# Gathered expert rows fetched three ahead into five buffers and taken earlier, with attention's keys in a pool of their own

## The chip, the cores and the metric

One core of one Trainium2 chip runs one decoder layer for 512 prompt positions and 8 x 8 sampled positions. The metric is the device time of one execution in microseconds (us). Three runs of the kernel before took 1851.71, 1856.73 and 1860.59 us; the median is 1856.73 us.

## The reference, cut to what matters

The layer has two halves. The first projects the input, runs a short convolution and a windowed attention side by side, merges both with sigmoid gates, and normalizes. The second retrieves experts: for each token 8 heads pick 16 of 16384 experts, and each expert is one row of `expert_u` (1024 numbers, a dot product with the token) and one row of `expert_v` (added to the output with a weight).

```
z = x @ w_in                     -> conv inputs, q, k, v, two gates
merged = sigmoid(g_conv) * (conv @ w_conv_out) + sigmoid(g_attn) * (attn @ w_attn_out)
h = layer_norm(ALPHA * x + merged @ w_o)
s = (h @ w_pq) . sub_keys        -> top 16 of each half, top 16 of the sums: idx, gate
coef = gate * gelu(h . expert_u[idx])
out = layer_norm(ALPHA * h + sum(coef * expert_v[idx]))
```

## The kernel before, in words

Five chunks of tokens are worked in two waves. Wave 0 (`first`) holds chunk 0 (128 prompt positions) and chunk SMP (64 sampled tokens, and 64 prompt positions whose experts go with chunk 3). Wave 1 (`second`) holds chunks 1, 2 and 3 with 128, 128 and 64 rows. Every weight table of 128x1024 goes through `table` (L136): one DMA to `raw`, the rounded part `whi` on ACT (L119), the rest `wlo` on POOL or DVE (L120), and three matmuls for each product (L123 to L125).

The stages in order of time are: wave 0 up to its norm; wave 1's queries, keys, convolution and attention, mixed with wave 0's top-16 search (`ORDER`, L62); wave 1's merges, `merge_conv` (L648, eight gated products written to `br` at L662) and `merge_attention` (L664, eight more, then `w_o` and the norm at L190 to L200); wave 1's search (`scores`, L733, 16 blocks of `w_pq`, each group followed by five `front`s); the gate matrix (L774, 96 `hot` tiles on DVE at L787, DMA to `gd`); and the dense experts.

The two groups of tokens find their experts in different ways. For wave 1's 384 rows (`DENSE`) all 128 tables of `expert_u` are multiplied (`front(t)`, L856), the first 60 results are spilled to DRAM, the last ten fronts before the gate matrix is finished (`KEEP`) are held back until the last `hot` matmul, and then `middle(t)` and `back(t)` (L898, L916) multiply by the gate matrix and accumulate 18 matmuls a table into six PSUM banks `acc` (L940). Fronts 69 to 127 run inside that last loop. For the chunks in `GATHER` (0 and SMP) the rows are gathered: `experts()` (L491) is a generator of 384 steps, 192 on `eu` and then 192 on `ev`. A step issues one indirect DMA of 512 KB from POOL (L512) into the ring of `GBUF` tiles `g`, `GLAG` steps ahead, and one DVE instruction on the row that has landed: L526 for `eu` (dot product into `pre`), L535 for `ev` (added to `h_tok`). From the end of wave 1's merges until the gate matrix is done, L526 reads the token's copy `hp` in PSUM (L486) and later `h` in SBUF. The PSUM of `hp` and of the other search tiles is closed at L889, and `acc` is opened in its place.

How many steps run when is set by `side(n)` behind a table's split: none in wave 1's search blocks, alternately 2 and 1 behind each front up to front 68, 1 behind each table of the back loop up to t = 59, 3 from t = 60, and what is left at the end. Instructions are put in order on each engine by a scheduler, so an engine takes them in one fixed order and waits at the head of its queue. Pools on one side of SBUF are a stack; a tile that is opened where a closed pool lay waits for that pool's last readers. The attention's `kT_all`, `v_all` and `mask_p` are constants here; `br` of wave 1 lies where wave 0's search input was.

Of the kernel before, what the change touches and what calls it, by code (L numbers as in the profile page):

```python
# [23 lines left out]
SEQ = 512  # L24
# [27 lines left out]
NS = 60  # L52
LAG = 9
AHEAD = NS + LAG
GBUF = 4
GLAG = 2
RAW = dict(w=3, v=3)
HI = dict(w=4, v=2)
OB = 3


ORDER = "qkscscasacsca"  # L62
# [1 line left out]
KEEP = 10  # L64
# [1 line left out]


PACE_N = 18
PACE_A, PACE_B, PACE_U, PACE_V = (1, 0), (2, 1, 1), (2, 1), (1, 3)
LO_N = 50  # L70
GATED = "aaag"
OUT = "aaav"
# [3 lines left out]
def step_kernel(ctx: ExitStack, tc: tile.TileContext, I: dict, O: dict):  # L76
    nc = tc.nc
    V, A, G, PE, S = nc.vector, nc.scalar, nc.gpsimd, nc.tensor, nc.sync

    pools = {}  # L80

    def pool(key, side, bufs=1):
        return tc.tile_pool(name=key, bufs=bufs, side=side)
# [8 lines left out]
    def psum(name, bufs):  # L92
        return tc.tile_pool(name=name, bufs=bufs, space=bass.MemoryType.PSUM)
# [8 lines left out]
    def tmp(p, shape, tag, name=None, bufs=1, dt=F32):  # L102
        return pools[p].tile(shape, dt, tag=tag, name=name or tag, bufs=bufs)

    loads, newest = [], [None, None]
# [6 lines left out]
    def const(name, shape, dtype=F32, src=None):  # L112
        t = pools["c"].tile(shape, dtype, tag=name, name=name)
        if src is not None:
            loads.append((t, src))
        return t
# [19 lines left out]
    def table(src, p, eng, pace=0):  # L136
        raw = tmp(p, [128, 1024], "raw", bufs=RAW[p])
        newest[0] = S.dma_start(raw, src).ins
        hi = tmp(p, [128, 1024], "whi", bufs=HI[p], dt=F32R)
        lo = tmp(p, [128, 1024], "wlo", bufs=HI[p], dt=F32R)  # L140
        last = split(hi, lo, raw, eng)
        if pace:
            with tc.issue_after(last.ins):
                side(pace)
        return hi, lo
# [14 lines left out]

    ident = const("ident", [128, 128])
    make_identity(nc, ident)
    mask_p = const("mask_p", [128, 256], src=I["mask_p"])
    convw = const("convw", [128, 4, 3], src=I["conv_w"])
    sink_p = const("sink_p", [128, 8], src=I["sink_p"])
    sink_s = const("sink_s", [128, 2, 2], src=I["sink_s"])
# [3 lines left out]
    ucar = const("ucar", [128, 4, 2])  # L170
    V.memset(ucar, 0.0)
    state = const("state", [128, 4, 8, 2], src=I["state"])
    kT_all = const("kT_all", [128, SEQ])
    v_all = const("v_all", [128, 5, 128])

    iota128 = const("iota128", [128, 128], src=I["iota128"])
    h_tok, idx, gate = {3: const("h3", [128, D])}, {}, {}
# [313 lines left out]
    def experts():  # L491
# [14 lines left out]
        def row():  # L506
            return tmp("g", [128, D], "g", bufs=GBUF)

# [5 lines left out]

        for i in range(GLAG):
            fetch(i)
        yield
        for i, (src, c, s) in enumerate(jobs):
            if i + GLAG < len(jobs):
                fetch(i + GLAG)  # L520
            g = rows.pop(i)
# [53 lines left out]
    def load_x(s):  # L575
        i, (a, b) = next(s.pieces)
        raw = tmp("g", [128, 1024], "g", bufs=GBUF)[:, :(b - a) * s.mv]
        S.dma_start(raw, I[f"xT{s.w}"][:, a * s.mv:b * s.mv])
        split(s.xT[0][:, a:b, :], s.xT[1][:, a:b, :], raw.rearrange("p (k n) -> p k n", n=s.mv), G if i == 1 else V)

    def weight(s, src):
        s.units += 1
        if s.w == 0:
            return table(src, "w", G if s.units % 3 != 1 else V)
        if s.units > LO_N:
            return table(src, "w", G)
        pace = PACE_A if s.units <= PACE_N else PACE_B
        if s.units % 4 == 3:
            return table(src, "w", V)
        return table(src, "w", G, pace[s.units % len(pace)])  # L590
# [35 lines left out]
    def attention(s, i):  # L626
# [7 lines left out]
        if c == SMP:  # L634
            kc = tmp("g", [128, 8, 128], "g", name="kc", bufs=GBUF)
            late(kc, I["kcT"])
            vc = tmp("g", [128, 8, 128], "g", name="vc", bufs=GBUF)
            late(vc, I["vc"])
# [171 lines left out]
    ks, bs = ExitStack(), ExitStack()  # L810
    pools["k"] = ks.enter_context(pool("k", "left"))
    pools["mm"] = ks.enter_context(psum("mm", 3))
    at_stack = ExitStack()
    pools["at"] = at_stack.enter_context(psum("at", 3))
    sel3 = ([tmp("k", [128, 128], f"k3{k}") for k in range(2)], tmp("k", [128, 128], "gt3"))
# [15 lines left out]
    for x in ORDER:  # L831
        do[x]()
        count[x] += 1
    first.rs.close()
    for dst, src in zip((*sel3[0], sel3[1]), (*first.sel[1][0], first.sel[1][1])):
        V.tensor_copy(dst[64:128], src[64:128])
    keys = {c: first.sel[i][0] for i, c in enumerate(GATHER)}
# [11 lines left out]
    scratch.append(shared[0])  # L849
    pools["hp"] = ks.enter_context(psum("hp", 1))  # L850
    pools["f"] = ctx.enter_context(pool("f", "right"))
    pools["b"] = bs.enter_context(pool("b", "right"))
    hT = second.hT
    coef = {}

    def front(t):  # L856
        wu = table(I["euT"][t], "w", G if t < AHEAD else V, PACE_U[t % len(PACE_U)] if t < AHEAD else 0)
        ps = bank("u")
        for k in range(8):
            mm3(ps[:, :ND], block(wu, k), (hT[0][:, k, :], hT[1][:, k, :]), k == 0, k == 7)  # L860
        if t < NS:
            ge = tmp("f", [128, ND], "sp", bufs=2)
            A.activation(ge, ps[:, :ND], AF.Gelu)  # L863
            S.dma_start(spill[t], ge)
        else:
            ge = tmp("f", [128, ND], "gel", bufs=LAG)
            A.activation(ge, ps[:, :ND], AF.Gelu)
            coef[t] = ge
# [3 lines left out]
    def fronts(n):  # L872
        nonlocal done
        while done < min(n, NE):
            front(done)
            done += 1

    for k, g4 in enumerate((0, 2, 1, 3)):
        scores(second, g4)
        fronts(FQ * (k + 1))  # L880
    total = len(DENSE) * 128 // GN
    base = done
    for i in range(len(DENSE)):
# [168 lines left out]
```

## Time and profile before

| what | us |
|---|---|
| median of three runs | 1856.73 |
| the profiled execution's own time | 1850.18 |
| its span, first to last instruction | 1848.4 |
| PE busy / DVE busy / POOL busy / ACT busy | 1723.9 / 1464.7 / 1109.6 / 781.4 |
| mean granted TensorE clock (share of full) | 0.972 |

The share of PE (93%) is a mean over stages with different limits, so a stage has to be read from its own stretch of the span. The profiled execution is 6.55 us under the median of the runs.

### The profile page before, as it was taken

The numbers are of one execution on the slowest core, as the hardware profiler recorded it, in microseconds if no ns is written. First come the engines' busy times: TensorE is split into PE (matmuls) and PEld (weight loads), VectorE is DVE, ScalarE is ACT, GpSimd is POOL, SyncE is SP. The second block draws the span as 40 slices with busy tenths as digits, with TensorE's granted clock in tenths as the row PEclk, the third lists the DMA queues.
The fourth block names the chain that finished last, engine by engine and source line by source line (L and its number), as shares of the span: only waits on it lengthen the run. The fifth ranks groups of instructions, "written<-read, shape, count | busy, mean of one in ns | idle before, by whom it ended". The sixth has DMA issues, their size and how long they took to land.

```text
span 1848.4 us, 27569 instructions
## 1 busy us (share of the span) xinstructions
PE 1723.9 (93%) x9760; PEld 1566.4 (85%) x9760; DVE 1464.7 (79%) x2588; ACT 781.4 (42%) x1337; POOL 1109.6 (60%) x724
## 2 busy tenths in 40 slices
PE   7999998998799999899888899999999999999985
PEld 7998898988489899799878778778999999999974
DVE  5634579998965699987893778779788878888887
ACT  4554444443233344377794333333333333343322
POOL 4445434367857777798645422224678787778783
PEclk9999999999989999899999999999999999999998
DMA  7446443368757789899748899999999999989873
GB/s 252 134 150 225 138 132 122 115 200 300 249 201 241 235 294 311 271 349 348 289 188 303 317 333 335 336 346 339 333 314 345 337 324 350 353 307 343 314 268 104
DMA packets 190539, 496.50 MB, mean 269 GB/s; under 512 B 17712, under 2 KB 83696, under 8 KB 187312
## 3 DMA queue, kind: packets, MB, share of 16 engines
q1 hardware_dynamic: 135104, 293.39, 46.5%
q0 software_dynamic: 55296, 201.35, 30.2%
q8 instruction: 76, 1.25, 0.3%
q14 instruction: 63, 0.52, 0.1%
HBM read 454.48 MB, written 40.54 MB: 268 GB/s over the span
## 4 chain that ended last, share of the span: by engine, by line
PE 40%; DVE 23%; DMA 14%; issue 9%; POOL 8%; ACT 4%; SPq 1%; DVEq 0%; POOLq 0%; ACTq 0%
PE acc L940 15%; PE ps L123 7%; PE ps L124 7%; PE ps L125 7%; DMA g<-in_ev,idx 5%; POOL wlo L120 4%; POOL g L512 4%; DVE junk L526 3%; PE ps L796 3%; DMA re<-spill 2%; DVE wlo L120 2%; DMA raw<-in_ev 2%; DMA raw<-in_w_o 1%; ACT whi L119 1%; ACT hot L793 1%
## 5 line engine op out<-in xcount | busy, mean ns | idle before, releaser
L120 POOL TENSOR_TENSOR wlo<-raw,whi 128x1024 fp32r<-128x1024 f32 x232 | 579.1, 2499 | 301.8 <-ACT whi L119 264.7
L119 ACT ACTIVATE whi<-raw 128x1024 fp32r<-128x1024 f32 x388 | 409.5, 1056 | 603.9 <-PE ps L124 236.1
L123 PE MATMUL ps<-xhi,whi 128*128 128x384 f32 (+2 forms) x1600 | 529.9, 331 | 21.6 <-ACT sp L863 13.4
L125 PE MATMUL ps<-xhi,wlo 128*128 128x384 f32 (+2 forms) x1600 | 526.1, 329 | 3.5 <-POOL wlo L120 2.0
L124 PE MATMUL ps<-xlo,whi 128*128 128x384 f32 (+2 forms) x1600 | 526.1, 329 | 0.0
L535 DVE SCALAR_TENSOR_TENSOR h<-g,pre,h 128x1024 f32<-128x1024 f32 x192 | 309.8, 1614 | 68.3 <-DMA g<-in_ev,idx 66.8
L512 POOL DMA_INDIRECT g<-in_eu,idx x192 | 204.2, 1063 | 233.1 <-DVE junk L526 186.9
L123 PEld LDWEIGHTS ps<-xhi,whi 128*128 128x128 f32 x1600 | 308.4, 193 | 31.0 <-ACT sp L863 15.1
L512 POOL DMA_INDIRECT g<-in_ev,idx x192 | 257.0, 1338 | 124.9 <-DVE h L535 77.9
L125 PEld LDWEIGHTS ps<-xhi,wlo 128*128 128x128 f32 x1600 | 307.8, 192 | 5.3 <-POOL wlo L120 2.3
L124 PEld LDWEIGHTS ps<-xlo,whi 128*128 128x128 f32 x1600 | 308.3, 193 | 2.9 <-issue 0.3
L940 PE MATMUL acc<-whi,chi 128*128 128x512 f32 x756 | 291.4, 392 | 14.5 <-ACT chi L119 8.2
L940 PE MATMUL acc<-wlo,chi 128*128 128x512 f32 x756 | 296.9, 393 | 7.6 <-POOL wlo L120 7.6
L940 PE MATMUL acc<-whi,clo 128*128 128x512 f32 x756 | 256.4, 392 | 1.1 <-DVE clo L120 1.1
L120 DVE TENSOR_TENSOR wlo<-raw,whi 128x1024 fp32r<-128x1024 f32 x156 | 203.5, 1304 | 46.0 <-ACT whi L119 43.6
L940 PEld LDWEIGHTS acc<-whi,chi 128*128 128x128 f32 x756 | 142.6, 189 | 46.7 <-ACT chi L119 11.5
L940 PEld LDWEIGHTS acc<-wlo,chi 128*128 128x128 f32 x756 | 142.4, 188 | 38.0 <-POOL wlo L120 9.7
L526 DVE SCALAR_TENSOR_TENSOR junk<-g,hp 128x1024 bf16<-128x1024 f32 x104 | 125.9, 1210 | 56.8 <-DMA g<-in_eu,idx 54.8
L940 PEld LDWEIGHTS acc<-whi,clo 128*128 128x128 f32 x756 | 142.4, 188 | 31.3 <-DVE clo L120 1.6
L526 DVE SCALAR_TENSOR_TENSOR junk<-g,h 128x1024 bf16<-128x1024 f32 x88 | 130.9, 1488 | 3.3 <-DMA g<-in_eu,idx 3.0
L796 PE MATMUL ps<-hot 128*128 128x128 f32 x768 | 113.4, 290 | 14.5 <-ACT hot L793 13.4
L787 DVE TENSOR_TENSOR hot<-pt,T 128x1024 f32<-128x1024 f32 x96 | 113.9, 1218 | 15.8 <-PE ps L796 12.7
(250 smaller groups left out, 2157.9 us busy)
## 6 DMA issues: line engine op xcount, KB each, us to landing
raw<-in_euT SPq DMA_DIRECT2D x128, 512.0 KB
raw<-in_ev SPq DMA_DIRECT2D x128, 512.0 KB
gd<-gb SPq DMA_DIRECT2D x24, 1024.0 KB
gm<-gd SPq DMA_DIRECT2D x48, 512.0 KB
raw<-in_w_g SPq DMA_DIRECT2D x32, 512.0 KB
raw<-in_w_pq SPq DMA_DIRECT2D x32, 512.0 KB
raw<-in_w_bch SPq DMA_DIRECT2D x24, 512.0 KB
spill<-sp SPq DMA_DIRECT2D x60, 192.0 KB
```

What stands on the lines that cost most here:

```text
L119: A.activation(hi, src, AF.Copy)
L120: return (eng or V).tensor_tensor(lo, src, hi.bitcast(F32), op=ALU.subtract)
L123: PE.matmul(ps, L[0], R[0], start=start, stop=False)
L124: PE.matmul(ps, L[0], R[1], start=False, stop=False)
L125: PE.matmul(ps, L[1], R[0], start=False, stop=stop)
L512: G.indirect_dma_start(out=rows[i], out_offset=None, in_=I[src], in_offset=bass.IndirectOffsetOnAxis(ap=idx[c][:, s:s + 1], axis=0))
L526: V.scalar_tensor_tensor(junk, g, 1.0, in_psum(c), op0=ALU.mult, op1=ALU.mult, accum_out=p)
L535: V.scalar_tensor_tensor(h_tok[c], g, p, h_tok[c], op0=ALU.mult, op1=ALU.add)
L787: V.tensor_tensor(hot, iota_ps.unsqueeze(1).unsqueeze(1).broadcast_to([128, 2, 4, 128]), T[:, 0:2, n:n + 4].unsqueeze(3).broadcast_to([128 ...
L793: A.activation(oi, oi, AF.Copy, scale=weight_of)
L796: newest[1] = PE.matmul(ps[:, r * 128:(r + 1) * 128], hot[:, 1, r, :], oi, start=True, stop=True).ins
L940: PE.matmul(*args, **kw)
```

## The change

Four things are done.

1. The ring of gathered rows has five tiles instead of four, and rows are fetched three steps ahead instead of two. The `hot` tiles go from three to four.
2. One step is added behind each of the 16 `w_pq` blocks of wave 1's search (`PACE_Q`), and the ten fronts that are kept back carry 3 steps each instead of 2 or 1: 16 and 15 steps earlier, 31 in all. The back loop keeps its paces, so it runs out of steps earlier.
3. `mask_p`, `kT_all` and `v_all` move from the constants to a pool `kv` that opens before wave 0 and closes when wave 1's attention is over.
4. The search's score tiles `sc` of wave 1 get a pool `b0`, closed before the gate matrix opens `b`.

```diff
-GBUF = 4
-GLAG = 2
+GBUF = 5
+GLAG = 3
-OB = 3
+OB = 4
-PACE_A, PACE_B, PACE_U, PACE_V = (1, 0), (2, 1, 1), (2, 1), (1, 3)
+PACE_A, PACE_B, PACE_Q, PACE_U, PACE_V = (1, 0), (2, 1, 1), 1, (2, 1), (1, 3)
-    mask_p = const("mask_p", [128, 256], src=I["mask_p"])
-    kT_all = const("kT_all", [128, SEQ])
-    v_all = const("v_all", [128, 5, 128])
         if s.units > LO_N:
-            return table(src, "w", G)
+            return table(src, "w", G, PACE_Q)
+    kvs = ExitStack()
+    pools["kv"] = kvs.enter_context(pool("kv", "left"))
+    mask_p, kT_all = tmp("kv", [128, 256], "mask_p"), tmp("kv", [128, SEQ], "kT_all")
+    v_all = tmp("kv", [128, 5, 128], "v_all")
+    loads.insert(0, (mask_p, I["mask_p"]))
     first.rs.close()
+    kvs.close()
-    pools["b"] = bs.enter_context(pool("b", "right"))
+    pools["b"] = bs.enter_context(pool("b0", "right"))
-        wu = table(I["euT"][t], "w", G if t < AHEAD else V, PACE_U[t % len(PACE_U)] if t < AHEAD else 0)
+        wu = table(I["euT"][t], "w", G if t < AHEAD else V, (PACE_U[t % len(PACE_U)] if t < AHEAD - KEEP else 3) if t < AHEAD else 0)
+    bs.close()
+    pools["b"] = bs.enter_context(pool("b", "right"))
```

Up to the fourth gate product of wave 1's `merge_conv` PE has the same order in both kernels. Behind it PE takes the last attention (chunk 3: transposes L297, sums L134, output L311). Here are its second transposes before; a matmul with 128x320 is a product of the merge.

```order
L124 MATMUL ps<-xlo,whi 128x320
L297 MATMUL ps<-ident,t_4083 128x64
L297 MATMUL ps<-ident,t_4083 64x64
L125 MATMUL ps<-xhi,wlo 128x320
L297 MATMUL ps<-ident,t_4083 128x64
L297 MATMUL ps<-ident,t_4083 64x64
L123 MATMUL ps<-xhi,whi 128x320
L124 MATMUL ps<-xlo,whi 128x320
L297 MATMUL ps<-ident,t_4083 128x64
L297 MATMUL ps<-ident,t_4083 64x64
```

The same transposes (now L294) on PE in the changed kernel, up to the next product of the merge:

```order
L294 MATMUL ps<-ident,t_4086 128x64
L294 MATMUL ps<-ident,t_4086 64x64
L131 MATMUL ps<-v_all,t_4105 64x64
L134 MATMUL ps<-v_all,t_4105 64x64 x7
L308 MATMUL ps<-ident,o 128x64 x4
L123 MATMUL ps<-chi,whi 128x320
L124 MATMUL ps<-clo,whi 128x320
```

Before, 179 products of the merge stand between the fourth gate product and the attention's last transposes; now none does, and all of them come behind.

On DVE, the end of the same attention before (`o`, L307, is its last step; `br`, L662, the merge's output):

```order
L662 TENSOR_TENSOR br<-cg,ps 128x320
L468 TENSOR_TENSOR rk<-rk,u_3911 128x64
L526 SCALAR_TENSOR_TENSOR junk,pre<-g,h_94 128x1024
L470 TENSOR_TENSOR oh<-rk,iota 128x1024
L526 SCALAR_TENSOR_TENSOR junk,pre<-g,h_94 128x1024
L307 TENSOR_TENSOR o<-ps,prd 64x4x64
L472 TENSOR_TENSOR oh<-oh,pf 128x1024
L662 TENSOR_TENSOR br<-bg,ps 128x320
```

And on DVE now (`o` at L304, `br` at L659):

```order
L523 SCALAR_TENSOR_TENSOR junk,pre<-g,h_91 128x1024
L470 TENSOR_REDUCE kk_2109<-oh 128x64
L304 TENSOR_TENSOR o<-ps,prd 64x4x64
L464 TENSOR_TENSOR rk<-rk,mk 128x64
L659 TENSOR_TENSOR br<-cg,ps 128x320
L659 TENSOR_TENSOR br<-bg,ps 128x320
L523 SCALAR_TENSOR_TENSOR junk,pre<-g,h_91 128x1024
```

Before, seven of the eight `br` stand ahead of the last `o`; now all eight stand behind it.

The third place is DVE behind the last `hot` tile, where the kept fronts run and the back loop begins. Before (`re` is a spilled result times the gate matrix, `wlo` a table of the back loop):

```order
L802 COPY gb<-ps 128x128x4
L910 TENSOR_TENSOR re<-re,gm 128x384 x2
L120 TENSOR_TENSOR clo<-re,chi 128x384 x2
L526 SCALAR_TENSOR_TENSOR junk,pre<-g,hp 128x1024
L910 TENSOR_TENSOR re<-re,gm 128x384
L526 SCALAR_TENSOR_TENSOR junk,pre<-g,hp 128x1024 x2
L910 TENSOR_TENSOR re<-re,gm 128x384 x2
L526 SCALAR_TENSOR_TENSOR junk,pre<-g,hp 128x1024
L120 TENSOR_TENSOR wlo<-raw,whi 128x1024
L526 SCALAR_TENSOR_TENSOR junk,pre<-g,hp 128x1024
L120 TENSOR_TENSOR wlo<-raw,whi 128x1024
L526 SCALAR_TENSOR_TENSOR junk,pre<-g,hp 128x1024 x2
```

On DVE now, from the third `re` on:

```order
L915 TENSOR_TENSOR re<-re,gm 128x384
L523 SCALAR_TENSOR_TENSOR junk,pre<-g,hp 128x1024 x3
L915 TENSOR_TENSOR re<-re,gm 128x384
L523 SCALAR_TENSOR_TENSOR junk,pre<-g,hp 128x1024
L915 TENSOR_TENSOR re<-re,gm 128x384
L523 SCALAR_TENSOR_TENSOR junk,pre<-g,hp 128x1024
L120 TENSOR_TENSOR wlo<-raw,whi 128x1024
L523 SCALAR_TENSOR_TENSOR junk,pre<-g,hp 128x1024 x2
L120 TENSOR_TENSOR wlo<-raw,whi 128x1024
L523 SCALAR_TENSOR_TENSOR junk,pre<-g,hp 128x1024 x2
L120 TENSOR_TENSOR wlo<-raw,whi 128x1024
L523 SCALAR_TENSOR_TENSOR junk,pre<-g,hp 128x1024
```

Behind these follow one more `wlo` and four more rows with `hp`: 7 rows that read `hp` stood behind the last `hot`, and now 15 do. In the same way the order has 21 rows before and 34 now between wave 1's norm and the third group's maxima, 39 and 46 from there to the first `hot`, and 36 and 39 among the `hot` tiles. The last gathered row stood five products' `clo` before the end of DVE's order and now stands ahead of the last eight tables' `gel`.

## Rows read from the trace of the kernel before

**Rows 1.** The page's chain that ended last, share of the span by engine.
```profile
PE 40%; DVE 23%; DMA 14%; issue 9%; POOL 8%; ACT 4%; SPq 1%; DVEq 0%; POOLq 0%; ACTq 0%
```

**Rows 2.** Windows: stretch, length, busy (count) by engine, PE clock, DMA share, GB/s.
```profile
core 0: us, PE busy (x) PEld busy (x) DVE busy (x) ACT busy (x) POOL busy (x), PEclk, DMA share, GB/s
400.00:450.00 50.00, 45.62 (x303) 43.12 (x301) 49.17 (x61) 14.89 (x23) 39.50 (x25) 1.00 0.88 291
...
1150.00:1200.00 50.00, 48.41 (x214) 39.75 (x213) 40.12 (x61) 18.76 (x25) 12.19 (x13) 1.00 0.95 331
```

**Rows 3.** The same view by stage, from wave 1's last attention to the last hot.
```profile
370.00:398.50 28.50, 26.39 (x161) 22.53 (x159) 28.44 (x84) 16.02 (x33) 13.86 (x8) 0.94 0.44 144
...
410.00:495.00 85.00, 77.03 (x413) 64.19 (x411) 75.45 (x92) 24.01 (x35) 64.95 (x38) 0.98 0.85 288
517.00:616.00 99.00, 98.85 (x609) 95.22 (x608) 48.07 (x202) 35.82 (x53) 69.32 (x41) 0.99 0.69 233
616.00:785.00 169.00, 153.30 (x860) 149.81 (x858) 164.05 (x526) 67.17 (x95) 126.11 (x78) 0.95 0.83 280
785.00:977.00 192.00, 177.68 (x1196) 170.30 (x1194) 166.29 (x191) 153.05 (x401) 135.26 (x148) 0.98 0.78 292
```

**Rows 4.** The same view, in the dense experts' loop.
```profile
1181.70:1202.40 20.70, 20.66 (x91) 17.13 (x92) 18.93 (x30) 7.61 (x10) 5.33 (x6) 1.00 0.91 312
```

**Rows 5.** The line of `br`: durations, first and last start, both waves.
```profile
L662 DVE TENSOR_TENSOR br<-cg,ps x8: 421/444/487, 83.5 to 400.4; 128x256 f32<-128x256 f32 x4, 128x320 f32<-128x320 f32 x4
```

**Rows 6.** DVE in order of time: the last attention's end, and the last `br`.
```profile
406.88 0.41 DVE L307 TENSOR_TENSOR o<-ps,prd 64x256 f32<-64x256 f32 x1
...
409.69 0.47 DVE L662 TENSOR_TENSOR br<-bg,ps 128x320 f32<-128x320 f32 x1
```

**Rows 7.** PE, 370 to 398.5: first and last of six groups of merge products; two in order.
```profile
L125 PE MATMUL ps<-xhi,wlo 128*128 128x320 f32 x25 | 8.9, 354 | 0.0
...
L125 PE MATMUL ps<-chi,wlo 128*128 128x320 f32 x15 | 4.6, 309 | 0.0
...
429.91 0.31 PE L123 MATMUL ps<-xhi,whi 128*128 128x320 f32 x1
430.06 0.31 PE L124 MATMUL ps<-xlo,whi 128*128 128x320 f32 x1
```

**Rows 8.** DVE in wave 1's search: its three longest waits for a row.
```profile
532.05 1.22 DVE L526 SCALAR_TENSOR_TENSOR junk<-g,hp 128x1024 bf16<-128x1024 f32 x1 [9.68 <-DMA g<-in_eu,idx]
...
571.09 1.22 DVE L526 SCALAR_TENSOR_TENSOR junk<-g,hp 128x1024 bf16<-128x1024 f32 x1 [14.31 <-DMA g<-in_eu,idx]
...
610.93 1.22 DVE L526 SCALAR_TENSOR_TENSOR junk<-g,hp 128x1024 bf16<-128x1024 f32 x1 [10.19 <-DMA g<-in_eu,idx]
```

**Rows 9.** Groups of DVE from 616 to 785: count, busy, mean ns, idle before.
```profile
L526 DVE SCALAR_TENSOR_TENSOR junk<-g,hp 128x1024 bf16<-128x1024 f32 x42 | 50.6, 1205 | 6.6 <-DMA g<-in_eu,idx 6.6
```

**Rows 10.** Behind the last hot: DVE, PE and POOL, each in order of time.
```profile
1031.87 1.22 DVE L526 SCALAR_TENSOR_TENSOR junk<-g,hp 128x1024 bf16<-128x1024 f32 x1
...
1033.31 0.77 PE L940 MATMUL acc<-whi,chi 128*128 128x512 f32 x1 [5.34 <-ACT whi L119]
...
1038.78 0.40 PE L940 MATMUL acc<-wlo,chi 128*128 128x512 f32 x1
...
1033.37 1.68 POOL L512 DMA_INDIRECT g<-in_eu,idx  x1 [0.33 <-DVE junk L526]
1035.65 1.68 POOL L512 DMA_INDIRECT g<-in_eu,idx  x1 [0.60 <-DVE junk L526]
```

**Rows 11.** The last of the back loop, columns as in rows 2.
```profile
1780.00:1830.00 50.00, 39.98 (x167) 30.34 (x166) 39.83 (x40) 12.79 (x18) 28.98 (x17) 1.00 0.55 180
```

**Rows 12.** DVE in order of time: the dense chunks' first step behind the last norm of a gathered chunk.
```profile
1827.08 1.27 DVE L947 SCALAR_TENSOR_TENSOR h<-h,acc 128x512 f32<-128x512 f32 x2
```

## The prediction

> **What bounds the kernel now.** I read the chain that ended last first: PE holds 40% of it and DVE 23% [rows 1], so no engine bounds the whole, and each stage has to be read by itself. The windows by stage show who sets the pace where. From 370 to 398.5 and from 400 to 450 DVE has no gap (28.44 of 28.50 us, 49.17 of 50) [rows 2, 3]. In wave 1's search PE is full (98.85 of 99) while DVE is idle for half of it; from there to the first `hot` DVE is the full one (164.05 of 169); among the `hot` tiles neither is (PE 177.68, DVE 166.29 of 192) [rows 3]. In the back loop PE is close to full: 48.41 of 50 us between 1150 and 1200, and 20.66 of 20.70 in a stretch without a wait [rows 2, 4]. At its end PE is not: 39.98 of 50 us from 1780 to 1830 [rows 11]. So rows that move into PE's search are free, rows that move into a stretch full on DVE are paid, and rows that leave the end of the loop pay back. The sum is made against the profiled execution, 1850.2 us, which stands 6.5 under the median of the runs.
>
> **Part A, the pool of the keys.** What this edit frees is SBUF; what it adds is a wait. `br` of wave 1 now lies where `kT_all`, `v_all` and `mask_p` lay, so no `br` may be written before the last attention has read them. Before, `br` began in the middle of that attention (the last `cg` of the eight starts at 400.4) [rows 5], and the orders show that 179 merge products, which filled PE while the softmax of the last attention ran, now come after it. A `br` that waits would hold DVE's queue, with the search and the attention's own steps behind it; the order avoids that by putting all eight behind the last `o`. What is lost is PE's cover. Of the 161 matmuls PE ran from 370 to 398.5 [rows 3], six groups of merge products make 119 (25, 24, 24, 16, 15, 15) [rows 7]; two such follow each other 0.15 us apart [rows 7], so about 17.5 us of PE work are pushed back. The last `o` ran at 406.88 and the last `br` at 409.69 [rows 6]; in the changed order some ten of DVE's long instructions (1.2 us each, an estimate) stand behind that `o` instead of ahead of it, so I put it at about 397. PE's lag is then 17.5 less some 1.5 us of attention matmuls that it ran after 398.5 and has now done. Four terms more: from 410 to 495 PE is idle for 8.0 of 85 us [rows 3], of which I take half as given back, 4; `w_o` now takes the chunk of 64 rows last and its norm can start earlier, which I estimate at 2.4 (half of some 5 us of DVE and ACT steps); and PE, idle for so long, comes back at half clock. The last is seen behind the last `hot`: after a wait of 5.34 us a matmul of 512 columns takes 0.63 to 0.77 us, and 0.40 five us later [rows 10]; the 13 matmuls between lose some 0.2 us each, 2.5 in all. 17.5 - 1.5 - 4 - 2.4 + 2.5 = 12.1; since DVE sets the pace of 400 to 450 and some of the lag will fall in its shadow, I take **+11**. The ends: all hidden but the clock, +2; nothing given back, 18.
>
> [...]
>
> **Part B, wave 1's search and the hots.** Of the steps moved forward, 13 more stand between wave 1's norm and the third group's maxima (21 before, 34 now). DVE has 51 us of idle time there [rows 3], 34 of them in three waits for a row that was fetched too late (9.68, 14.31, 10.19) [rows 8], while a row costs 1.22 [rows 8]: 16 us into 51 of idle time. PE has no gap there, and I cost the rows at nothing; if that cover were gone it would be 16. Seven more stand from there to the first `hot`, where DVE is full: 7 x 1.285 (1.205 [rows 9] and some 0.08 for a read against POOL's port, an estimate) = 9.0. Among the `hot` tiles three more make 3.9, but PE has 1.8 fronts less to do there, since they run earlier (7.6 us, where the 20.66 us of 91 matmuls hold five tables' work [rows 4]), both engines have slack (14.3 and 25.7 of 192) [rows 3], and the fourth `hot` tile lets DVE run ahead, for which I take 1.3: 3.9 - 7.6 - 1.3 = -5. Together **+4**. The ends: -4, since the deeper ring also removes 6.6 us in which DVE waited for a row where it is full [rows 9]; +13, with no gain among the hots.
>
> **Part C, the kept fronts.** The order puts 15 rows with `hp` on DVE behind the last `hot`, where 7 stood. They matter because of what follows: `acc` opens its six PSUM banks where `hp` lies, so the first `acc` matmul must wait for the last row that reads `hp`. The trace shows it: that row ends at 1031.87 + 1.22 = 1033.09, and the first `acc` matmul starts at 1033.31 after 5.34 us of idle time [rows 10]. (The view names `whi` as the releaser; it had been done earlier.) Eight rows more at 1.29 are 10.3, and two more `wlo` at about 1.22 stand ahead, 2.4: 12.7 on DVE. POOL issues rows here at a pace of 2.28 us (1033.37 to 1035.65) [rows 10], so eight rows that wait on the ring would cost 18. Taken away from that: part falls in gaps of DVE, and the loop that follows can give something back where it is not full: from 1150 to 1200 it runs 214 matmuls where the pace of 91 in 20.70 us allows 220 [rows 2, 4], so 3% of some 250 us, 7 at most, of which I take 2. **+11**; the ends 5 and 18.
>
> **Part D, the end.** 31 steps leave the back loop's end, where three steps a table set the pace. There PE is idle for 10.0 us from 1780 to 1830 [rows 11]; without rows PE runs at its own pace, -10. The first step of the dense chunks' output starts at 1827.08, behind the last norm of a gathered chunk [rows 12]; with that norm done earlier another 1.5 is won. **-11.5**; the ends -13 and -7 (some of PE's gaps have other causes).
>
> A landed row waits longer in a fuller ring, and POOL issues the same number of DMAs on the same queue, only earlier; `sc` in its own pool closes before the gate matrix needs its place. I cost both at nothing: POOL is idle for 30 us of the search's 99 [rows 3].
>
> **The sum.** 11 + 4 + 11 - 11.5 = +14.5: 1850.2 + 14.5 = 1864.7 in the profile's terms, and 1871 with the 6.5 to the median.
>
> **The rivals.** (1) Not slower: PE's lag is absorbed. DVE has 49.17 of 50 us of work from 400 to 450 [rows 2], and if the norm is set by DVE and not by the merge, A is 0, and the sum +3.5: 1860. It decides as soon as A is under about 6. For it speaks the full DVE; against it that PE has 77.03 of 85 us of its own there, only 8 to give [rows 3]. (2) The first `acc` matmul doesn't hang on the `hp` rows but on a table's load; then C is some 3 and the sum +6.5: 1863. Against it, the 0.2 us between the two [rows 10]. (3) Faster: the change does what an earlier fetch can do. The waits for rows in the full stretch go (6.6 us [rows 9]) and the rows moved forward are taken in DVE's idle time, so B is -5, A is hidden, C is 3 or 4, and D is whole: 0 - 5 + 4 - 11.5 = -12.5, 1844. It decides if DVE after the search starts ahead of its present time. Against it, the order still puts seven rows more into that full stretch. (4) The end gives nothing back: PE's gaps there come from the loads of tables or from POOL, D is -2, and the sum +24: 1881. Against it, DMA is at 0.55 of its share there [rows 11].
>
> **How the numbers follow.** My forecast has 0.50, the rivals 0.20, 0.10, 0.08 and 0.12. The forecast's own range is 1860 to 1883, by about half of the ends of A, B and C going the same way. Adding rivals (1), (2) and (4) and dropping the faster one, I take 1853 to 1886. 0.5% is 9.3 us, about what a measurement of this kernel can tell from no change. Over 1866 counts as slower: two thirds to three quarters of the forecast, nearly all of (4), a quarter of the others: 0.58. From 1847.4 to 1866: most of (1) and (2) and a quarter of the forecast: 0.32. Below: (3) and a little of (1): 0.10.
>
> **What would show it.** In the changed kernel's trace: A, PE idle between about 370 and 398 and at half clock after it, with `w_o` ending 8 to 14 us later than before; if `w_o` ends as before, A is wrong. B, the three long waits for rows in the search gone, and the first `hot` some 9 us later against wave 1's norm. C, from the last `hot` to the first `acc` matmul 10 to 15 us more. D, PE without gaps in the last 50 us of the back loop, and that end about 11 us shorter. A forecast of slower falls if A and C together come to under 10 us.

## The result, and the profile after

The changed kernel takes 1870.94 us (median of 13 runs, 1862.6 to 1880.3) against 1852.03 us of the kernel before (13 runs): ratio 1.0094, 95% interval 1.0073 to 1.0115, so +17.4 us. In a second comparison it was 1.0129 (1.0091 to 1.0168). The prediction was 1871, that is +14.5; the two profiled executions of the changed kernel have spans of 1862.4 and 1876.1 us, 14.0 and 27.7 over the 1848.4 of before.

To see where the time went I took six points of the program in every profile: the first matmul of wave 1's search, the start of the first and of the last `hot`, the first `acc` matmul, the 1700th `acc` matmul (in table 94, where the loop runs at PE's own pace, 40.00 of 40 us busy from 1590 to 1630 in the changed kernel; in every profile 840 matmuls of fronts stand between it and the first), and the end. Differences to the profile of before, in us:

| stretch | predicted | changed | changed, second profile |
|---|---|---|---|
| start to first search matmul (A) | +11 | +10.3 | +22.0 |
| to first `hot` (B) | +9 | +4.4 | +3.2 |
| first to last `hot` (B) | -5 | -5.0 | -6.7 |
| to first `acc` matmul (C) | +13 | +11.8 | +12.8 |
| first 94 tables of the back loop | -2 | +8.3 | +12.3 |
| rest (D) | -11.5 | -15.8 | -15.8 |
| sum | +14.5 | +14.0 | +27.7 |

The page's chain that ended last, shares by engine, which answers to [rows 1]: PE has 54% of it instead of 40%.

```profile
PE 54%; DVE 21%; DMA 10%; issue 5%; ACT 4%; POOL 4%; SPq 1%; DVEq 0%; ACTq 0%; POOLq 0%
```

The windows of the changed kernel's profile that answer to [rows 2, 3, 11] (stretch, length, busy time and count of PE, PE's weight loads, DVE, ACT and POOL, granted clock, DMA share, GB/s); the last two are the stretch from the last `hot` to the first `acc` matmul, 57.82 us before, and the last of the back loop.

```profile
370.00:398.50 28.50, 15.45 (x71) 10.05 (x70) 27.43 (x90) 8.01 (x25) 9.77 (x9) 0.60 0.51 171
410.00:495.00 85.00, 78.39 (x453) 71.03 (x452) 66.65 (x86) 27.13 (x39) 69.08 (x37) 0.96 0.81 281
...
985.17:1054.78 69.61, 48.40 (x265) 46.58 (x264) 31.61 (x44) 20.89 (x34) 39.65 (x29) 0.88 0.92 327
...
1800.00:1850.00 50.00, 48.33 (x218) 40.21 (x216) 15.46 (x29) 15.17 (x22) 14.63 (x7) 1.00 0.15 51
```

The first row shows part A: 71 matmuls instead of 161, PE idle for nearly half of the time and at a mean granted clock of 0.60 (0.70 up to 384, 0.50 from there to 396.5), while DVE is as full as before. The second shows that PE had little to give back afterwards: 6.6 of 85 us idle, 8.0 before. The last shows part D: PE, which was idle for 10 us there, is now idle for 1.7.

DVE at the last attention's end, in order of time:

```profile
395.68 0.40 DVE L304 TENSOR_TENSOR o<-ps,prd 64x256 f32<-64x256 f32 x1
396.14 0.47 DVE L659 TENSOR_TENSOR br<-cg,ps 128x320 f32<-128x320 f32 x1
```

And PE behind it, the merge's first products:

```profile
396.76 0.63 PE L123 MATMUL ps<-chi,whi 128*128 128x320 f32 x1
397.19 0.47 PE L124 MATMUL ps<-clo,whi 128*128 128x320 f32 x1
...
399.57 0.31 PE L124 MATMUL ps<-clo,whi 128*128 128x320 f32 x1
```

The last `o` runs at 395.68 (I had put it at 397) and the first `br` 0.46 us behind it. PE then takes 0.47 us for a product at a mean granted clock of 0.51 (396.76 to 399.57), and 0.31 us at 1.00 behind that (to 402).

DVE's last row with `hp`, which answers to the first line of [rows 10]:

```profile
1053.35 1.22 DVE L523 SCALAR_TENSOR_TENSOR junk<-g,hp 128x1024 bf16<-128x1024 f32 x1 [0.80 <-DMA g<-in_eu,idx]
```

And PE's first `acc` matmuls, which answer to the next line there:

```profile
1054.78 0.77 PE L945 MATMUL acc<-whi,chi 128*128 128x512 f32 x1 [14.45 <-issue]
1055.35 0.63 PE L945 MATMUL acc<-wlo,chi 128*128 128x512 f32 x1
```

The row ends at 1054.57 and PE starts at 1054.78, 0.2 us behind it as before, but after 14.45 us of idle time instead of 5.34. No semaphore is named for that wait ("issue").

### The profile page after: what moved, and what is told of

The parts are those of the page before. It is cut to its first block, busy times and chain, and to the rows that moved or that the text cites. A ratio compares the mean times of both kernels' runs of the same rounds, so it can differ in the third digit from the quotient of the medians.

```text
span 1862.4 us, 27605 instructions
## 1 busy us (share of the span) xinstructions
PE 1727.8 (93%) x9760; PEld 1572.6 (84%) x9760; DVE 1464.2 (79%) x2588; ACT 777.8 (42%) x1335; POOL 1113.1 (60%) x724
## 4 chain that ended last, share of the span: by engine, by line
PE 54%; DVE 21%; DMA 10%; issue 5%; ACT 4%; POOL 4%; SPq 1%; DVEq 0%; ACTq 0%; POOLq 0%
PE acc L945 23%; PE ps L123 9%; PE ps L124 9%; PE ps L125 9%; DVE junk L523 4%; POOL wlo L120 3%; PE ps L793 3%; DMA re<-spill 2%; DMA raw<-in_ev 2%; ACT whi L119 1%; ACT hot L790 1%; DVE s L409 1%; DMA raw<-in_w_o 1%; DVE oh L467 1%; DVE wlo L120 1%
## 5 line engine op out<-in xcount | busy, mean ns | idle before, releaser
L120 POOL TENSOR_TENSOR wlo<-raw,whi 128x1024 fp32r<-128x1024 f32 x232 | 588.7, 2539 | 358.3 <-ACT whi L119 341.9
L123 PE MATMUL ps<-xhi,whi 128*128 128x384 f32 (+2 forms) x1600 | 529.0, 331 | 15.7 <-ACT sp L866 7.5
L509 POOL DMA_INDIRECT g<-in_ev,idx x192 | 249.7, 1301 | 184.2 <-DVE h L532 129.4
L532 DVE SCALAR_TENSOR_TENSOR h<-g,pre,h 128x1024 f32<-128x1024 f32 x192 | 292.8, 1525 | 28.5 <-DMA g<-in_ev,idx 27.1
L523 DVE SCALAR_TENSOR_TENSOR junk<-g,hp 128x1024 bf16<-128x1024 f32 x135 | 163.5, 1211 | 43.7 <-DMA g<-in_eu,idx 39.7
L945 PEld LDWEIGHTS acc<-whi,chi 128*128 128x128 f32 x756 | 143.5, 190 | 59.8 <-ACT chi L119 16.5
L793 PE MATMUL ps<-hot 128*128 128x128 f32 x768 | 112.3, 292 | 14.2 <-ACT gb L797 6.2
L784 DVE TENSOR_TENSOR hot<-pt,T 128x1024 f32<-128x1024 f32 x96 | 113.0, 1215 | 13.5 <-PE ps L793 10.7
L793 PEld LDWEIGHTS ps<-hot 128*128 128x128 f32 x768 | 105.0, 199 | 20.2 <-ACT hot L790 11.8
```

Source lines behind the costliest of these rows:

```text
L120: return (eng or V).tensor_tensor(lo, src, hi.bitcast(F32), op=ALU.subtract)
L123: PE.matmul(ps, L[0], R[0], start=start, stop=False)
L509: G.indirect_dma_start(out=rows[i], out_offset=None, in_=I[src], in_offset=bass.IndirectOffsetOnAxis(ap=idx[c][:, s:s + 1], axis=0))
L523: V.scalar_tensor_tensor(junk, g, 1.0, in_psum(c), op0=ALU.mult, op1=ALU.mult, accum_out=p)
L532: V.scalar_tensor_tensor(h_tok[c], g, p, h_tok[c], op0=ALU.mult, op1=ALU.add)
L784: V.tensor_tensor(hot, iota_ps.unsqueeze(1).unsqueeze(1).broadcast_to([128, 2, 4, 128]), T[:, 0:2, n:n + 4].unsqueeze(3).broadcast_to([128 ...
```

## What the first 60 tables of the back loop lost

This is the one stretch in which the sign was wrong. PE waits there in both profiles for a `chi`, at three tables above all: 3.28, 1.56 and 3.24 us at tables 18, 34 and 50 in the first, 2.42, 4.45 and 3.44 at the same three in the second. (The first profile has 2.09 at table 41 too; before, no wait of the loop behind its first matmul is over 1.59.) Here is ACT at table 18, in order of time. `chi` is the rounded part of what PE needs now; the three `whi` are those of tables 19, 20 and 21, counted by the four buffers that `whi` has:

```profile
1123.56 1.06 ACT L119 ACTIVATE whi<-raw 128x1024 fp32r<-128x1024 f32 x1 [0.67 <-PE acc L945]
1130.02 1.06 ACT L119 ACTIVATE whi<-raw 128x1024 fp32r<-128x1024 f32 x1 [5.40 <-DMA raw<-in_ev]
1133.45 1.06 ACT L119 ACTIVATE whi<-raw 128x1024 fp32r<-128x1024 f32 x1 [2.37 <-DMA raw<-in_ev]
1134.41 0.51 ACT L119 ACTIVATE chi<-re 128x384 fp32r<-128x384 f32 x1
```

And PE, whose first matmul of that table waited for this `chi`:

```profile
1134.97 0.50 PE L945 MATMUL acc<-whi,chi 128*128 128x512 f32 x1 [3.28 <-ACT chi L119]
```

Three `whi` stand on ACT's queue ahead of the `chi` of table 18, and two of them wait 5.40 and 2.37 us for a table's load. ACT's queue is only half of it. This `chi` needs DVE's `re` of table 18, and on DVE that `re` stands behind the `wlo` of table 20, which waits for the second of the three `whi`:

```profile
1131.11 1.23 DVE L120 TENSOR_TENSOR wlo<-raw,whi 128x1024 fp32r<-128x1024 f32 x1 [3.43 <-ACT whi L119]
...
1133.40 0.55 DVE L915 TENSOR_TENSOR re<-re,gm 128x384 f32<-128x384 f32 x1
```

The `re` ends at 1133.95 and the `chi` starts at 1134.41, so another order of ACT alone could have gained 0.5 us here; the split of table 20 stands ahead of the work of table 18 on both engines. What is late is table 20's load: it was issued at 1122.05, behind three loads of the gate matrix (`gm`, 512 KB each, from 1115.75 on). Such loads come every eight tables in every kernel, and waits of PE at tables two behind a multiple of eight show before too (0.76 us at table 10, 1.59 at table 34); they are long where the order has a triple.

The order of the changed kernel has such a triple at tables 18, 34 and 50 and nowhere else behind the loop's start; the order of before has pairs, but no triple. Nothing in the diff speaks of this place: the scheduler sets these orders for the whole program, and an edit elsewhere shifts them.

```
chi<-re
whi<-raw
chi<-re x2
whi<-raw x3
chi<-re x3
whi<-raw x2
```

That is ACT's order in the changed kernel around table 18 (names only); in a smooth stretch `whi` and `chi` take turns.

The waits are not the whole loss. Behind the 4.45 us at table 34 of the second profile PE's matmuls take 0.63 us each instead of 0.39 for most of the table:

```profile
1216.86 0.79 PE L945 MATMUL acc<-whi,chi 128*128 128x512 f32 x1 [4.45 <-ACT chi L119]
1217.45 0.63 PE L945 MATMUL acc<-wlo,chi 128*128 128x512 f32 x1
...
1223.73 0.39 PE L945 MATMUL acc<-whi,chi 128*128 128x512 f32 x1
```

In the first profile the same is seen behind the waits of 2.09 and 3.24 us (0.63 us a matmul, at a mean granted clock of 0.52 from 1235.7 to 1238.9 and 0.50 from 1276.77 to 1279.9), and not behind that of 3.28 (1.00 from 1135 to 1138.2).

From the first to the 1700th `acc` matmul PE is idle for 13.8 and 14.9 us in the two profiles (8.2 before) and busy for 540.8 and 543.6 (538.1 before): of the 8.3 and 12.3 us lost, 5.6 and 6.7 are waits, and 2.7 and 5.5 are matmuls that took longer. The experiments below fit this, though none of them changes the order alone.

## The experiments

All ratios are against the kernel before, run beside it on the same chip.

**The keys' pool alone.**

```diff
-    mask_p = const(...); kT_all = const(...); v_all = const(...)
+    pools["kv"] = kvs.enter_context(pool("kv", "left"))
+    mask_p, kT_all, v_all = tmp("kv", ...)
...
+    kvs.close()
```

> The kernel before with one part of the change: mask_p, kT_all and v_all in the pool that closes behind wave 1's last attention. Paces, ring and hot tiles stay. My theory: PE loses its cover under the last attention and the first search matmul of wave 1 (512 to 527 us) starts about 10 us later (516.4 before), with nothing given back later, so about +10 us in all (ratio 1.005). Rival 'absorbed': DVE sets the stretch from 400 to 495, the first search matmul starts within 3 us of before, and the time is the same (ratio under 1.002).

Measured: 1.0125 (1.008 to 1.017), +23 us, twice what I expected. First search matmul +13.5, as the theory said; but the first 94 tables of the back loop took 11.9 us more, which nothing had led me to expect. A second time, to see whether that was one execution:

> The kernel before with the keys' pool alone, a second time, since it came out at +23 us (ratio 1.0125) while the same with the deeper ring came out at +5, and the stretch that the pool should touch (to the first search matmul) had 11 to 15 us more. Theory 'the pool costs 15, the rest was that execution': first search matmul at 526 to 535 us, the first 60 tables of the back loop as in the kernel before, +15 in all (ratio 1.006 to 1.010). Rival 'the ring earns beside the pool': +20 or more again, with the loss in the first 60 tables again.

Measured: 1.0119 (1.0082 to 1.0157), with +12.0 to the first search matmul and +15.5 in the back loop. So the loss belongs to the kernel, and the theory that it was one execution fell. PE's long waits lie at tables 10, 26 and 42 (3.72, 2.74, 3.92; second time 3.40, 4.33, 4.22), and the order of this kernel has its triples of `whi` at tables 10, 26, 42 and 58. Here is ACT at table 10 in the first of the two:

```profile
1084.41 1.06 ACT L119 ACTIVATE whi<-raw 128x1024 fp32r<-128x1024 f32 x1 [5.86 <-DMA raw<-in_ev]
1087.82 1.06 ACT L119 ACTIVATE whi<-raw 128x1024 fp32r<-128x1024 f32 x1 [2.35 <-DMA raw<-in_ev]
1088.78 0.93 ACT L119 ACTIVATE chi<-re 128x384 fp32r<-128x384 f32 x2
```

It is the same picture at another table: on DVE the `re` of table 10 stands behind a `wlo` that waited 4.55 us. Paces, ring and instructions in that loop are those of before, and their order is not; 12 to 16 us go with it. (The tiles' places in SBUF differ as well, and no run separates the two.)

**The keys' pool with the deeper ring.**

```diff
+    (the keys' pool as above)
-GBUF, GLAG = 4, 2
+GBUF, GLAG = 5, 3
```

> The kernel before with the keys' pool and the deeper ring (five buffers, three ahead), paces and hot tiles as before. Against the kernel with the keys' pool alone (+20) this shows the ring by itself. Theory 'the ring costs' (the changed kernel with the old ring was 10 us faster than with the new one): about +28 (ratio 1.015), and the loss lies behind the first acc matmul, in the first 60 tables of the back loop. Rival 'the ring costs only where rows are taken early': +20 (1.011). Rival 'the ring earns' (it removes waits for rows): +14 or less.

Measured: 1.0026 (1.0005 to 1.0047), +5 us, the last of the three theories. The first search matmul is still 14.1 us later, but the back loop is 4.2 us faster than before instead of 12 to 16 slower; its order has no triple, and but for pairs near table 18 `whi` and `chi` take turns, as here at table 11:

```profile
1093.34 0.53 ACT L119 ACTIVATE chi<-re 128x384 fp32r<-128x384 f32 x1 [1.57 <-PE acc L943]
1093.77 1.05 ACT L119 ACTIVATE whi<-raw 128x1024 fp32r<-128x1024 f32 x1
```

Here ACT waits for PE, not for a load. Behind the loads of `gm` it waits for a table's load in this kernel too (8.89 us at table 26, 8.47 at table 34), but with one `whi` ahead of the `chi`, and PE waits 1.77 and 1.72.

**The changed kernel with the ring of before.**

```diff
-GBUF, GLAG = 5, 3
+GBUF, GLAG = 4, 2
```

> The changed kernel with the ring of before (four buffers, two ahead); keys' pool, paces and hot tiles as changed. My theory: the ring is worth little either way, within 4 us of the changed kernel: +11 to +18 against before (ratio 1.006 to 1.010). Rival 'the ring costs': rows fetched further ahead are what slows the first 60 tables of the back loop, and the 8 us lost there go: +6 to +9 (1.004). Rival 'the ring earns': the waits for rows in the search and among the hots come back, +20 or more (1.012).

Measured: 1.004 (1.0012 to 1.0069), +7 us, 10 less than the changed kernel, as the rival 'the ring costs' said. But beside the kernel with keys and ring (18 less with the ring than without) the sign is the opposite, so the ring itself has no fixed price. What goes along with both is the order of the back loop: no triple and +3.0 us there in this kernel, three and +8.3 or +12.3 in the changed one. A second difference is in both pairs the same: with the deeper ring the stretch from the first to the last `hot` is 5 to 6 us longer (-11.4 here, -5.0 and -6.7 in the changed kernel; -1.7 with the keys alone, +3.9 with keys and ring). DVE's idle time ahead of its `hot` instructions is 4.8 us here and 13.5 in the changed kernel, 10.7 of it ended by PE's reading of an earlier tile; why the deeper ring brings these waits back was not tried.

**The search's steps alone.**

```diff
-            return table(src, "w", G)
+            return table(src, "w", G, PACE_Q)
```

> The kernel before with one step behind each of the 16 w_pq blocks, nothing else. 18 rows more stand ahead of the first hot, the last row of the back loop comes seven tables earlier. My theory: the rows are nearly free in the search (first hot 0 to 5 us later), and the end of the loop gains what the changed kernel gained there in part, 8 to 13 us: about -7 us in all (ratio 0.996). Rival 'early ev': the loss of 8 us that the changed kernel shows in the back loop's first 60 tables comes from the ev rows, which begin earlier there; then this kernel shows some 4 of it too, and -3 us in all. Rival 'rows are paid where DVE is full': first hot 9 us or more later, and no gain.

Measured: 0.9956 (0.9932 to 0.998), -8 us; the theory said -7. The first `hot` comes 3.0 us later against the first search matmul, for 18 rows more; the end gains 5.8. The back loop is 3.4 us faster, so ev rows that begin earlier are not what it lost.

**Two steps behind each block.**

```diff
-            return table(src, "w", G)
+            return table(src, "w", G, 2)
```

> The kernel before with two steps behind each of the 16 w_pq blocks, nothing else: 25 more rows ahead of the first hot, seven more among the hots, the last row 13 products' clo before the end of DVE's order (2 before, 9 with one step). My theory: the end of the loop gains 15 (7 with one step), the search loses 3 to 6 and the hots 0 to 5: about -8 us (ratio 0.996), no more than with one step. Rival 'DVE's idle time covers them all': -15 (0.992). Rival 'rows are paid where DVE is full': first hot 12 us later, and 0 in all.

Measured: 1.0011 (0.9989 to 1.0033), no gain left. The first `hot` is 16.9 us later: 25 rows more are 32 us, and DVE's idle time covers only half of them; the end gains 11.9. The seven rows that the second step adds to the 18 of the first cost 13.9 us, more than their own 9, and why is open. So one step behind a block is nearly free and the second is paid; the rival 'paid where DVE is full' holds from there.

**The kept fronts' steps alone.**

```diff
-    ... PACE_U[t % len(PACE_U)] if t < AHEAD else 0
+    ... (PACE_U[t % len(PACE_U)] if t < AHEAD - KEEP else 3) if t < AHEAD else 0
```

> The kernel before with 3 steps behind each of the ten kept fronts, nothing else; 16 rows that read hp stand behind the last hot (7 before). My theory: from the last hot to the first acc matmul takes 70 us instead of 59, +11; the end of the loop gains 8 to 13; about 0 in all (ratio 1.000, between 0.997 and 1.003). Rival 'acc does not hang on the hp rows': 60 to 62 us for that stretch, and -8 us in all (0.996).

Measured: 1.0126 (1.0087 to 1.0165), +23 us where I expected none. The mechanism is as expected, the size not: from the last `hot` to the first `acc` matmul +15.2 for nine rows and two `wlo` more, the `hot` tiles +4.7 with six rows more and only three `hot` buffers, and the end gains 1.0, though its last row stands as early as that of the kernel with the search's steps, which gained 5.8. In this profile PE also waits 3.2 us for tables between 1625 and 1667, which takes part of that gain; the rest stays open. The stretches of this profile add up to 16.8, and its execution lies 7.6 us under the median of its runs.

**Both paces and the fourth hot tile, with constant keys and the old ring.**

```diff
-GBUF, GLAG = 5, 3
+GBUF, GLAG = 4, 2
-    (the keys' pool)
+    (the keys as constants)
```

> The changed kernel with mask_p, kT_all and v_all as constants again and the ring of before (four buffers, two ahead; the fifth needs the room of the keys' pool), so both paces and the fourth hot tile alone. My theory: the terms add up, and this is the changed kernel with the old ring less the 11 us of the lost cover: first search matmul at 516 to 524 us as in the kernel before, about -4 us in all (ratio 0.998, between 0.993 and 1.002). Rival 'the sum of the single edits': search alone gave -9 and the kept fronts alone +22, so +13 (1.007).

Measured: 0.9955 (0.9931 to 0.998), -8 us. Against the changed kernel with the old ring, which differs from it in the keys' pool alone, it is 15.7 us faster (7.4 + 8.3, by the two intervals some 7 either way). ACT has the same triple-free order there in both, so this is the price of the pool's wait by itself. The sum of the single edits (+13) falls with it.

**The fourth hot tile.**

```diff
-OB = 3
+OB = 4
+    PACE_Q = 1, and the score tiles in a pool b0 of their own
```

> The kernel before with one step behind each w_pq block and four hot tiles (the search's score tiles in a pool of their own, so that they fit); kept fronts, ring and keys as before. Against the kernel with the search's steps alone (-8) it shows the fourth hot tile. My theory: the fourth tile takes DVE's waits for PE among the hots away (191 us from the first to the last hot in the kernel before, 188 with the search's steps, 180 in the two kernels with four tiles and the old ring), 6 to 8 us less: -15 in all (ratio 0.992). Rival 'the gain among the hots is that of the fronts that run earlier with the kept pace': 188 us there, and -8 (0.9955).

Measured: 0.9905 (0.9873 to 0.9938), -17.6 us, 9.5 more than the search's steps alone (by the two intervals some 8 either way): my theory, and a little more. The first to the last `hot` takes 175.67 us (192.13 before, 189.16 with the search's steps). The group of the `hot` instructions on DVE over that stretch in the kernel with the search's steps and three tiles (count, busy time, mean ns, idle time before and what ended it):

```profile
L787 DVE TENSOR_TENSOR hot<-pt,T 128x1024 f32<-128x1024 f32 x94 | 111.9, 1218 | 19.1 <-PE ps L796 8.8 <-ACT hot L793 4.1 <-ACT T L780 2.3
```

And in the kernel with four:

```profile
L787 DVE TENSOR_TENSOR hot<-pt,T 128x1024 f32<-128x1024 f32 x95 | 111.1, 1215 | 5.2 <-ACT T L780 2.7 <-PE ps L796 1.5 <-ACT hot L793 0.6
```

DVE's idle time ahead of its `hot` instructions falls from 19.1 to 5.2 us, the part that PE's reading ends from 8.8 to 1.5.

**No steps behind the kept fronts.** First with two steps behind each block, then with one and four hot tiles.

```diff
-    ... PACE_U[t % len(PACE_U)] if t < AHEAD else 0
+    ... PACE_U[t % len(PACE_U)] if t < AHEAD - KEEP else 0
```

> The kernel before with two steps behind each w_pq block and none behind the ten kept fronts: no row that reads hp stands behind the last hot (7 before, 15 in the changed kernel). My theory: the first acc matmul hangs on those rows, so the stretch from the last hot to it takes 50 to 54 us instead of 59, the end of the loop gains 7, the search loses 3: about -12 us (ratio 0.9935). Rival 'behind the rows the loads of the tables are next': 57 to 59 us for that stretch, and about -6 in all.

Measured: 0.9966 (0.9947 to 0.9986), -6 us; the first `acc` matmul 13.1 us earlier against the last `hot`, with 16.0 lost ahead of the first `hot` by the doubled steps, as above.

> As the kernel with the search's steps and four hot tiles, and no step behind the ten kept fronts: no row that reads hp behind the last hot, eight fewer among the hots, and the last row seven tables later again. My theory: the first acc matmul 13 us earlier, the end of the loop 7 to 10 us later, so -4 against that kernel and -18 against before (ratio 0.990). Rival 'the rows are paid at the end in full': -8 (0.9955).

Measured: 0.983 (0.9793 to 0.9867), -32 us, better than both kernels. The stretch from the last `hot` to the first `acc` matmul takes 44.55 us instead of 57.82, with no wait of PE in it:

```profile
964.65:1009.20 44.55, 44.41 (x260) 44.02 (x259) 18.01 (x17) 18.86 (x31) 22.39 (x12) 1.00 0.87 296
```

And its first `acc` matmul on PE:

```profile
1009.20 0.39 PE L942 MATMUL acc<-whi,chi 128*128 128x512 f32 x1
```

PE has 44.41 of 44.55 us in that window (columns as above), at full clock; the first `acc` matmul takes 0.39 us and waited for nothing. The rows come back at the end (+3.8 there instead of -3.7), far less than they had cost. The stretches of this profile add up to -18.4, which is the forecast; its execution lies 7.1 us above the median of its runs, and the rest of the -32 is not located.

**The changed kernel a second time.**

> The changed kernel a second time, for a second profile of the same instructions and a second ratio beside the other kernels. Theory: +17 (ratio 1.007 to 1.0115), with the terms of the first profile: first search matmul 10 to 15 us later, hots 4 less, first acc matmul 11 more, the end of the loop 15 less. What is open: whether the 8 us that the first profile lost in the first 60 tables of the back loop come again (then they belong to the change), or not (then they were that execution).

Measured: 1.0129 (1.0091 to 1.0168). The loss in the first 94 tables came again, 12.3 us, at the same three tables: it belongs to the change.

The same table as above for all of them, differences to the profile of before in us (columns: to the first search matmul; to the first `hot`; to the last `hot`; to the first `acc` matmul; to the 1700th; to the end), then the ratio:

| kernel | search | hot | hots | acc | loop | end | ratio |
|---|---|---|---|---|---|---|---|
| keys | +13.5 | -2.2 | -1.7 | -0.5 | +11.9 | -1.5 | 1.0125 |
| keys, second | +12.0 | +1.7 | -1.7 | -1.0 | +15.5 | +0.1 | 1.0119 |
| keys, ring | +14.1 | +5.8 | +3.9 | -5.9 | -4.2 | -4.4 | 1.0026 |
| changed, old ring | +18.5 | +7.0 | -11.4 | +15.4 | +3.0 | -14.6 | 1.0040 |
| search | +7.9 | +3.0 | -3.0 | +0.5 | -3.4 | -5.8 | 0.9956 |
| search twice | -9.6 | +16.9 | +2.0 | 0.0 | -1.7 | -11.9 | 1.0011 |
| kept | +1.1 | -3.1 | +4.7 | +15.2 | -0.1 | -1.0 | 1.0126 |
| paces, four hots | +3.3 | +4.4 | -11.8 | +13.9 | -1.0 | -14.2 | 0.9955 |
| search, four hots | +3.8 | +3.4 | -16.5 | +0.1 | +1.3 | -3.7 | 0.9905 |
| search twice, kept 0 | -7.4 | +16.0 | -1.9 | -13.1 | +3.3 | -7.0 | 0.9966 |
| search, four hots, kept 0 | +1.6 | +7.5 | -19.9 | -13.3 | +1.9 | +3.8 | 0.9830 |

In the column of the loop the four profiles with a triple have +8.3 to +15.5, and the ten without one (that of before among them) -4.2 to +3.3. The longest wait of PE there without a triple is 3.21 us, at table 50 of the kernel with doubled steps and none behind the kept fronts.

A row adds up to the difference of two single executions, which lies up to some 13 us from what the ratio says. The first column needs care: eight kernels have no keys' pool and the same order on PE and DVE up to that point, and their first search matmul ran between 506.8 and 524.3 us (mean 516.5). With the pool, six profiles gave 526.7 to 538.3 (mean 531.4). One profile doesn't measure this term to better than about 9 us; the two groups don't overlap, and their means are 14.9 apart.

## Why the prediction was right, and where it was not

Time and sign were right: +14.5 forecast, +17.4 and +24 measured, 1871 against 1870.94. It is partly luck: the loop came out 10 to 14 us dearer than forecast, and the rows ahead of the first `hot` and the end some 5 and 4 us cheaper. That the two times agree to 0.1 us is luck too, since the 6.5 that was added led to the median of three runs of the kernel before (1856.73), and its 13 runs beside the changed kernel have 1852.03.

**Part A held, and was sized low.** Forecast +11, measured 14.9 between the groups of profiles and 15.7 between the two kernels that differ in the pool alone. Nothing of it was absorbed by DVE, so rival (1) falls, though DVE is the full engine there: the lag was PE's, and PE had no gap to take it up. The term that was mis-sized is the 4 us that I took as given back from 410 to 495: the idle time there went from 8.0 to 6.6, so 1.4 came back; with it the sum is 12.1 + 2.6 = 14.7. That fits the runs, but no run tests this term by itself. The lower clock shows on the merge's first ten matmuls, 2.8 us at a mean granted 0.51 instead of some 1.5 at the pace behind them: about 1.3, less than the 2.5 taken. The trace has a mean granted clock of 0.60 in the stretch with PE half idle (370 to 398.5), then these products of 0.47 us, and products of 0.31 us at 1.00 behind them; before, the clock granted behind the last `hot` was 0.50 from 1033.31 to 1038.54.

**Part B was right on the hots, too high ahead of them.** The three waits of 9.68, 14.31 and 10.19 us [rows 8] are gone; the longest one now is 4.99. The rows cost +4.4 and +3.2 where I had 9, so some of the seven still found idle time. (No run shows the 0.08 as a read against POOL's port: what the traces show is an instruction of its own, a DVE_READ_ACCUMULATOR behind the rows, 0.08 us in the mean in both kernels.) Among the hots I had -5, and -5.0 and -6.7 came. That sum came out, its terms didn't: I had credited the fourth tile with 1.3 and the fronts that run earlier with 7.6. By the runs the tile is worth 13.5 (-16.5 against -3.0), the kept fronts' six rows more cost 5 (-11.8 against -16.5), and the deeper ring takes 5 to 6 back.

**Part C was right.** Forecast +13 to the first `acc` matmul, measured +11.8 and +12.8; the 0.2 us between the last `hp` row and the matmul [rows 10] came again, and in the kernel with four hot tiles and no such rows PE doesn't wait there at all (44.41 of 44.55 us busy). Rival (2) falls. The `whi` that the view of before named as its releaser was not it.

**The step that failed is the 2 us that the loop would give back.** The prediction asked only what the loop would gain from a late start, and costed the rows' DMAs at nothing because POOL had time. It asked who issues the DMAs and never in which order DVE and ACT take the halves of two tables. The loop lost 8.3 and 12.3 instead: at three tables the split of a table two ahead, late from its load, stands on DVE ahead of the `re` and on ACT ahead of the `chi` that PE needs, and behind some of these waits PE's matmuls take 0.63 us instead of 0.39 (at a granted clock of 0.50 at table 50 of the first profile), which was counted for part A alone. The order shows it without a run, but I had read it only at the places of the edits. That the order is the cause rests on the waits and on which kernels have the triple; no run changes it alone.

**Part D held, with more.** Forecast -11.5, measured -15.8 twice: 12.5 in the last tables and 3.3 behind them, where I had 1.5. Rival (4) falls. Rival (3) was closer than its chance of 0.08 said: the kernel without the keys' pool and the ring is faster by 8 us; what kept the change from it is A, the loop's order and the ring's 5 to 6 us among the hots.

## What to carry to other kernels

A pool that closes early saves room only if nothing that opens on its place was used as cover for its last readers: look at what the waiting engine did during that stretch before. When work is moved by a scheduler, read the orders of every queue in the stages where an engine is close to full, far from the edit too: work for the next tables that waits for a load, put ahead of what is needed now, went with 8 to 16 us here, as much as an edit. And a buffer's reader counts as part of the stage that follows when the next stage opens on the same place: eight rows on `hp` and two `wlo` more delayed `acc` by 11.8 and 12.8 us.

## What the runs showed of the hardware that was not expected

Executions differ ahead of the first search matmul by up to 17 us (506.8 to 524.3 us in eight profiles with the same order on PE and DVE up to there; 526.7 and 538.3 in the two of the changed kernel), while the loop behind the 60th table agrees from one profile of a kernel to the next to 0.1 us (from the 1071st to the 1700th `acc` matmul both profiles of the changed kernel take 288.4 us). A stage's price from a single profile is as good as that stage repeats, and no better.
